# An elementwise Huber loss in larger tiles: three slots and a quarter in place of two pairs of slots

## The chip, the core and the metric

The kernel runs on one core of one Trainium2 chip. The metric is the device time of one execution in microseconds (us), lower being better. The kernel before takes 1868.55 us, the median of three runs (1867.75 to 1868.61).

## The reference

`pred` and `target` are float32 arrays of 8192 x 8192, and so is the result:

```
diff = pred - target
abs_diff = np.abs(diff)
np.where(abs_diff <= 1.0, 0.5 * diff**2, abs_diff - 0.5)
```

With m for `diff` clamped to -1 to 1, the result is also max(|diff| - 0.5, 0.5 m m); both kernels compute it in that form. Every element of two arrays is read once and every element of a third is written once: 805.3 MB in all.

## The kernel before

The arrays are flattened and seen as 128 partitions by 524288 columns in all. They are cut into tiles of 128 x 13248 (`W`, line 25); what is left over, 128 x 7616, is the first tile (lines 28 to 30). That is 40 tiles. Within a tile each partition holds one run of consecutive elements (`block`, line 34), so a row of a full tile is 52992 bytes.

On-chip memory holds two slots for `pred` (`a0`, `a1`) and two for `target` (`b0`, `b1`), each of a tile's width (lines 38 to 40). Tile i uses slot i mod 2 of each.

`load(i)` (line 49) issues the transfers of both inputs, through line 53. A middle tile has one transfer of `pred` and one of `target`. The first two tiles, and the second and third from the end, have their loads cut in two halves; the last has four quarters of each (lines 55 to 62). `store(i)` (line 67) writes the result from the `target` slot through line 70, in one transfer, and the last tile's in five. All transfers, loads and stores, are issued by SP, in the order in which the program states them. SP waits at each for what it needs: the store for the last result, a load for its slot.

`compute(i)` (line 72) cuts a middle tile into three pieces of 4416 columns. For each piece there are five instructions:

- line 92, DVE: a = a - b
- line 93, DVE: b = a clamped to -1 to 1
- line 96, ACT: b = 0.5 b b (a square with a scale)
- line 97, ACT: a = |a|
- line 86, DVE: b = max(a - 0.5, b), put off until two further pieces have been started (`finish(2)`), the last of a tile after its last piece

The order on each engine is that of the program text (`manual_schedule`, line 102). The main loop computes tile i, issues its store, and then the loads of tile i + 2 into the same slots (lines 104 to 110):

```
load(0)
load(1)
for i in range(n):
    compute(i)
    store(i)
    if i + 2 < n:
        load(i + 2)
```

The load of `pred` i + 2 needs slot `a` of tile i, whose last reader is line 86 of tile i. The load of `target` i + 2 needs slot `b` of tile i, whose last reader is the store of tile i, so SP waits there until that store has landed.

Of the kernel before, what the change touches and what calls it, by code (L numbers as in the profile page):

```python
# [1 line left out]

# [4 lines left out]


@with_exitstack
def kernel(  # L10
    ctx: ExitStack,
    tc: tile.TileContext,
    pred: bass.AP,
    target: bass.AP,
    out: bass.AP,
):
    nc = tc.nc
    P = 128
    fp32 = mybir.dt.float32
    Alu = mybir.AluOpType  # L20
    Act = mybir.ActivationFunctionType
    SQRT_HALF = 0.70710678118654752

    total = pred.shape[0] * pred.shape[1] // P
    W = 13248
    H, Q, E = W // 2, W // 4, W // 8

    widths = [W] * (total // W)
    if total % W:
        widths.insert(0, total % W)  # L30
    n = len(widths)
    starts = [sum(widths[:i]) * P for i in range(n)]

    def block(x, i):
        flat = x.rearrange("r m -> (r m)")
        return flat[starts[i] : starts[i] + P * widths[i]].rearrange("(p m) -> p m", p=P)

    pool = ctx.enter_context(tc.tile_pool(name="slots", bufs=1))
    a_slots = [pool.tile([P, W], fp32, name=f"a{k}") for k in range(2)]
    b_slots = [pool.tile([P, W], fp32, name=f"b{k}") for k in range(2)]  # L40

    def cuts(pieces):
        at, found = 0, []
        for w in pieces:
            found.append(slice(at, at + w))
            at += w
        return found

    def load(i):
        a, b = a_slots[i % 2], b_slots[i % 2]  # L50

        def get(dst, src, c):
            nc.sync.dma_start(out=dst[:, c], in_=block(src, i)[:, c])  # L53

        if i == n - 1:
            c = cuts([Q] * 4)
            order = [(0, 0), (0, 1), (1, 0), (1, 1), (0, 2), (1, 2), (0, 3), (1, 3)]
            for which, k in order:
                get((a, b)[which], (pred, target)[which], c[k])
            return  # L60
        w = widths[i]
        pieces = [w // 2] * 2 if i in (0, 1, n - 3, n - 2) else [w]
        for c in cuts(pieces):
            get(a, pred, c)
            get(b, target, c)

    def store(i):
        pieces = [Q] * 3 + [E] * 2 if i == n - 1 else [widths[i]]
        for c in cuts(pieces):
            nc.sync.dma_start(out=block(out, i)[:, c], in_=b_slots[i % 2][:, c])  # L70

    def compute(i):
        if i == n - 1:
            pieces = [E] * 8
        elif i == n - 2:
            pieces = [Q] * 4
        elif i == 0:
            pieces = [widths[0] // 2] * 2
        else:
            pieces = [W // 3] * 3  # L80
        todo = []

        def finish(keep):
            while len(todo) > keep:
                a, b = todo.pop(0)
                nc.vector.scalar_tensor_tensor(  # L86
                    out=b, in0=a, scalar=-0.5, in1=b, op0=Alu.add, op1=Alu.max
                )

        for c in cuts(pieces):  # L90
            a, b = a_slots[i % 2][:, c], b_slots[i % 2][:, c]
            nc.vector.tensor_tensor(out=a, in0=a, in1=b, op=Alu.subtract)  # L92
            nc.vector.tensor_scalar(  # L93
                out=b, in0=a, scalar1=-1.0, scalar2=1.0, op0=Alu.max, op1=Alu.min
            )
            nc.scalar.activation(out=b, in_=b, func=Act.Square, scale=SQRT_HALF)  # L96
            nc.scalar.activation(out=a, in_=a, func=Act.Abs)  # L97
            todo.append((a, b))
            finish(2)
        finish(0)  # L100

    ctx.enter_context(tc.manual_schedule())

    load(0)
    load(1)
    for i in range(n):
        compute(i)
        store(i)
        if i + 2 < n:
            load(i + 2)  # L110


# [1 line left out]
_INS = ['pred', 'target']  # L114
_OUTS = [((8192, 8192), 'float32')]


# [23 lines left out]
```

## Time and profile before

| what | value |
|---|---|
| median of 3 runs | 1868.55 us |
| span of the profiled execution, first to last instruction | 1867.4 us |
| DVE busy | 1406.2 us, 75% |
| ACT busy | 903.9 us, 48% |
| bytes moved, and mean rate over the span | 805.37 MB, 431 GB/s |
| transfers issued by SP | 138 |
| packets, counting one per partition row and one per transfer and DMA engine that signals its end | 19879, 2208 of them under 512 B |

For the profiled execution the profile gives the span of its instructions and no time of its own beside it, so the 1.15 us between the span and the median of the other runs is carried along as a constant.

The 138 transfers fit the packets: 138 x 128 rows are 17664, 138 x 16 engines are 2208, and 7 packets fetch instructions.

How to read it: the second part of the page cuts the span into 40 slices and shows the busy share of each engine and of the 16 DMA engines. Where one row is full in every slice, that row sets the time, and the others show how much cover there is. The timeline lists instructions in order of time; an instruction of the form `SPq ... DMA_DIRECT2D` is the moment at which SP hands a transfer to the DMA engines, not the transfer itself. The idle time in square brackets at an instruction names what ended it.

### The profile page before, as it was taken

How to read it: one execution, taken by the hardware profiler on the slowest of the kernel's cores; microseconds unless marked ns; L12 is line 12 of the kernel's file. 1: busy time of each engine (PE TensorE's matmuls, PEld its weight loads, DVE VectorE, ACT ScalarE, POOL GpSimd, SP SyncE). 2: the span in 40 equal slices, each digit the busy share in tenths (PEclk: the TensorE clock that was granted, in tenths of full speed). 3: DMA queues.
4: the chain of work that ended last, by engine and by line, in shares of the span. 5: the costliest groups of instructions: out<-in, count | busy, mean ns of one | idle time of the engine just before them, and what ended most of it. 6: DMA issues, size and time to landing. Idle time of an engine off the chain costs nothing.

```text
span 1867.4 us, 994 instructions
## 1 busy us (share of the span) xinstructions
DVE 1406.2 (75%) x375; ACT 903.9 (48%) x251; POOL 0.2 (0%) x4
## 2 busy tenths in 40 slices
DVE  5677777777777777777777777777777777777886
ACT  3444444444444444444444444444444444444454
POOL 0000000000000000000000000000000000000000
DMA  9999999999999999999999999999999999999999
GB/s 412 423 432 436 436 431 433 436 432 431 428 435 434 435 432 432 432 435 434 434 434 435 432 434 432 435 434 432 436 434 432 434 434 432 432 436 430 432 429 390
DMA packets 19879, 805.37 MB, mean 431 GB/s; under 512 B 2208, under 2 KB 2208, under 8 KB 2464
## 3 DMA queue, kind: packets, MB, share of 16 engines
q1 hardware_dynamic: 19872, 805.32, 99.9%
q14 instruction: 7, 0.06, 0.0%
HBM read 536.87 MB, written 268.44 MB: 431 GB/s over the span
## 4 chain that ended last, share of the span: by engine, by line
DMA 61%; DVE 37%; issue 0%; SPq 0%; DVEq 0%
DMA b<-in_target_dram 33%; DMA out_dram<-b 28%; DVE b L86 15%; DVE a L92 15%; DVE b L93 8%; SPq L53 0%; DVEq L136 0%; DVEq L92 0%
## 5 line engine op out<-in xcount | busy, mean ns | idle before, releaser
L96 ACT ACTIVATE b<-b 128x4416 f32<-128x4416 f32 (+3 forms) x125 | 461.1, 3688 | 945.6 <-DVE b L93 945.6
L92 DVE TENSOR_TENSOR a<-a,b 128x4416 f32<-128x4416 f32 (+3 forms) x125 | 565.4, 4523 | 439.2 <-DMA b<-in_target_dram 439.2
L86 DVE SCALAR_TENSOR_TENSOR b<-a,b 128x4416 f32<-128x4416 f32 (+3 forms) x125 | 558.6, 4521 | 2.7 <-ACT a L97 2.7
L97 ACT ACTIVATE a<-a 128x4416 f32<-128x4416 f32 (+3 forms) x125 | 460.3, 3682 | 0.0
L93 DVE TENSOR_SCALAR b<-a 128x4416 f32<-128x4416 f32 (+3 forms) x125 | 293.1, 2344 | 4.3
L96 ACT ACT_TABLE_LOAD x1 | 1.3, 1283 | 0.7 <-PEq L125 0.7
L125 POOL MEMSET const-bfloat16-1.0<- 128x1 bf16 x1 | 0.1, 102 | 0.0
L125 POOL MEMSET const-uint8-127<- 128x1 uint8 x1 | 0.1, 101 | 0.0
L125 POOL MEMSET const-float32-0.0<- 128x1 f32 x1 | 0.1, 99 | 0.2 <-issue 0.2
L125 POOL MEMSET const-float32-1.0<- 128x1 f32 x1 | 0.1, 98 | 0.0
## 6 DMA issues: line engine op xcount, KB each, us to landing
out_dram<-b SPq DMA_DIRECT2D x38, 6624.0 KB, 26.9
a<-in_pred_dram SPq DMA_DIRECT2D x35, 6624.0 KB, 42.1
b<-in_target_dram SPq DMA_DIRECT2D x35, 6624.0 KB, 31.3
a<-in_pred_dram SPq DMA_DIRECT2D x6, 3312.0 KB, 30.4
b<-in_target_dram SPq DMA_DIRECT2D x6, 3312.0 KB, 30.5
a<-in_pred_dram SPq DMA_DIRECT2D x4, 1656.0 KB, 31.6
b<-in_target_dram SPq DMA_DIRECT2D x4, 1656.0 KB, 18.6
out_dram<-b SPq DMA_DIRECT2D x3, 1656.0 KB, 18.9
```

What stands on the lines that cost most here:

```text
L86: nc.vector.scalar_tensor_tensor(out=b, in0=a, scalar=-0.5, in1=b, op0=Alu.add, op1=Alu.max)
L92: nc.vector.tensor_tensor(out=a, in0=a, in1=b, op=Alu.subtract)
L93: nc.vector.tensor_scalar(out=b, in0=a, scalar1=-1.0, scalar2=1.0, op0=Alu.max, op1=Alu.min)
L96: nc.scalar.activation(out=b, in_=b, func=Act.Square, scale=SQRT_HALF)
L97: nc.scalar.activation(out=a, in_=a, func=Act.Abs)
L125: nc = _bacc.Bacc("TRN2", target_bir_lowering=False, num_devices=1)
```

## The change

The tiles become 128 x 16256 (`W` = 4 `Q`, `Q` = 4064), 31 of them, with a first tile of 13568 columns and a last of 6784: 33 tiles. On-chip memory is one buffer of 3 `W` + `Q` columns. `target` (and the result) of even tiles lies at 0, of odd tiles at `W`. There is one region for `pred`, at 2 `W` for even tiles and `Q` columns further for odd ones, so that the `pred` regions of neighbouring tiles overlap in three quarters. The first tile's `pred` lies at `W`, where the `target` of tile 1 comes later.

The subtraction now writes into the `target` region (`d` = pred - target there). For a middle tile all four subtractions, 4064 columns each, come first (`subtract_all`), the quarter that no later transfer needs last. Then SP may load the next `pred` tile over the freed region, and the rest of the tile, eight pieces of 2032 columns (`loss`), works in the `target` region and in a quarter that is free meanwhile (`scratch`), which has room for two clamped pieces. Line 100 (the former line 86) is put off by one piece (`finish(1)`), not two.

For a middle tile the built program has SP wait, ahead of the load of the next `pred`, for the third of the four subtractions: for tile 1 these are the instructions 25 to 28 that DVE signals, and SP waits for 27. The order on SP is: store of tile i - 1, `pred` of i + 1, `target` of i + 1. That `target` load still waits until the store of tile i - 1 has landed. Transfers are 108 in number: 4 loads each for the first and the last two tiles, 2 for each of 30 others, and 36 stores.

```diff
-    W = 13248
+    Q = 4064
+    W = 4 * Q
+    middle = 31
+    first = 13568
+    widths = [first] + [W] * middle + [total - first - middle * W]
...
+    mem = pool.tile([P, 3 * W + Q], fp32, name="mem")
+    def at_a(i):
+        if i == 0:
+            return W
+        if i == n - 1:
+            return at_a(n - 2)
+        return 2 * W + (Q if i % 2 else 0)
+    def at_b(i):
+        return W if i % 2 else 0
+    def scratch(i):
+        following = min(i + 1, n - 2)
+        return 2 * W if at_a(following) != 2 * W else 3 * W
...
+    def subtract(i, c):
+        a, b = view(at_a(i), c), view(at_b(i), c)
+        nc.vector.tensor_tensor(out=b, in0=a, in1=b, op=Alu.subtract)
...
+    def loss(i, c):
+        finish(1)
+        d = view(at_b(i), c)
+        t = view(scratch(i) + turn[0] * (Q // 2), (0, c[1] - c[0]))
+        turn[0] ^= 1
+        nc.vector.tensor_scalar(
+            out=t, in0=d, scalar1=-1.0, scalar2=1.0, op0=Alu.max, op1=Alu.min
+        )
+        nc.scalar.activation(out=t, in_=t, func=Act.Square, scale=SQRT_HALF)
+        nc.scalar.activation(out=d, in_=d, func=Act.Abs)
+        todo.append((d, t))
...
+    def subtract_all(i):
+        order = [1, 2, 3, 0] if at_a(i) == 2 * W else [0, 1, 2, 3]
+        for k in order:
+            subtract(i, (k * Q, k * Q + Q))
...
     load(0)
-    load(1)
-    for i in range(n):
-        compute(i)
-        store(i)
-        if i + 2 < n:
-            load(i + 2)
+    load_pred(1, (0, W))
+    work_on_part(0, 0)
+    work_on_part(0, 1)
+    finish(0)
+    load_target(1, (0, W))
+    for i in range(1, n - 2):
+        store(i - 1)
+        subtract_all(i)
+        load(i + 1)
+        for c in cuts(even(W, 8)):
+            loss(i, c)
+        if i < n - 3:
+            finish(0)
+    work_on_part(n - 2, 0)
+    store(n - 3)
+    load(n - 1)
+    work_on_part(n - 2, 1)
+    work_on_part(n - 1, 0)
+    store(n - 2, even(W, 2))
+    work_on_part(n - 1, 1)
+    finish(0)
+    h = 1696
+    store(n - 1, [widths[n - 1] // 2, widths[n - 1] // 2 - h, h])
```

`work_on_part(i, k)` subtracts and treats half k of a tile piece by piece (pieces of 1696 columns in the first and last tile, of 2032 in the last but one); the tiles at both ends are worked so. The last tile is stored in 3392, 1696 and 1696 columns.

## The prediction

> **What bounds it now.** I read the page first: busy shares by slice and the chain that ended last.
>
> ```profile
> DVE  5677777777777777777777777777777777777886
> ACT  3444444444444444444444444444444444444454
> POOL 0000000000000000000000000000000000000000
> DMA  9999999999999999999999999999999999999999
> GB/s 412 423 432 436 436 431 433 436 432 431 428 435 434 435 432 432 432 435 434 434 434 435 432 434 432 435 434 432 436 434 432 434 434 432 432 436 430 432 429 390
> ...
> DMA 61%; DVE 37%; issue 0%; SPq 0%; DVEq 0%
> ```
>
> The DMA row is full in all 40 slices, while DVE is never above 8 tenths. The chain names DVE for 37%, but only because store and load hang on it in turn; a full DMA row means that the queue held other work meanwhile. The timeline of one steady tile shows this:
>
> ```profile
> 602.43 0.34 SPq L70 DMA_DIRECT2D out_dram<-b  x1
> 602.91 0.34 SPq L53 DMA_DIRECT2D a<-in_pred_dram  x1
> 613.83 4.76 DVE L92 TENSOR_TENSOR a<-a,b 128x4416 f32<-128x4416 f32 x1 [11.42 <-DMA b<-in_target_dram]
> ...
> 629.41 0.33 SPq L53 DMA_DIRECT2D b<-in_target_dram  x1
> ...
> 649.44 0.34 SPq L70 DMA_DIRECT2D out_dram<-b  x1
> 650.27 0.33 SPq L53 DMA_DIRECT2D a<-in_pred_dram  x1
> 660.77 4.76 DVE L92 TENSOR_TENSOR a<-a,b 128x4416 f32<-128x4416 f32 x1 [11.35 <-DMA b<-in_target_dram]
> ```
>
> The store is issued 11.4 us before the target load ahead of it has landed (602.43, 613.83); the wait for the store ends at 629.41, 15.58 us after that landing, and pred is already queued. From landing to landing (613.83 to 660.77) three transfers take 46.94 us, 15.647 each, with no gap. So only three things can move the time: what each transfer costs beside its bytes, gaps that the new order opens, and both ends.
>
> **Price of a transfer.** The start shows a smaller size:
>
> ```profile
> 0.73 0.37 SPq L53 DMA_DIRECT2D a<-in_pred_dram  x1
> ...
> 12.55 4.12 DVE L92 TENSOR_TENSOR a<-a,b 128x3808 f32<-128x3808 f32 x1 [12.55 <-DMA b<-in_target_dram]
> ...
> 21.62 4.13 DVE L92 TENSOR_TENSOR a<-a,b 128x3808 f32<-128x3808 f32 x1 [2.76 <-DMA b<-in_target_dram]
> ```
>
> Two transfers of 3808 columns take 21.62 - 12.55 = 9.07 us, 4.535 each. With 15.647 us for 13248 columns, a column costs 11.112 us / 9440 = 1.1771 ns and a transfer 0.05 us more. The same rows price a start from an empty queue: 12.55 - 9.07 = 3.48, which is 2.75 us from the first issue (0.73) to where transfer time begins, counting the way to DVE at the landing.
>
> All columns cost 3 x 524288 x 1.1771 ns = 1851.4 us; 138 transfers add 6.9; the start is 3.48; after the data the span goes on some 0.9 us (the last packets fall in 1865 to 1866, by windows of 1 us). Together 1862.7. The span is 1867.4, so 4.7 us are stalls of the slowest DMA engine. They lie early: the five pairs of tiles between the target issues at 110.37 and 582.48 (chain of waits) take 472.1 us, the five after it (582.48 to 1051.80) 469.3, that is 0.28 us more per tile.
>
> **The change, part by part.**
>
> *Fewer transfers.* 138 become 108: 30 x 0.05 = **-1.5 us**. On the full queue nothing hides this.
>
> *Early stalls.* The trace does not say what makes them. If they come per tile, 33 tiles for 40 leave 4.7 x 33/40 = 3.9, **-0.8 us**; bounds: all vanish (-4.7), or the early 0.28 us for each of 33 tiles (9.2, +4.5). I take -0.8, nearest to what this order of load and store showed.
>
> *The new wait.* Now pred i + 1 cannot queue until three subtractions of tile i are done; the queue then holds only the store of i - 1. Prices by these rows:
>
> ```profile
> L92 DVE TENSOR_TENSOR a<-a,b 128x4416 f32<-128x4416 f32 x111 | 527.7, 4754 | 413.9 <-DMA b<-in_target_dram 413.9
> ...
> L92 DVE TENSOR_TENSOR a<-a,b 128x1656 f32<-128x1656 f32 x8 | 15.0, 1876 | 2.5 <-DMA b<-in_target_dram 2.5
> L86 DVE SCALAR_TENSOR_TENSOR b<-a,b 128x1656 f32<-128x1656 f32 x8 | 14.8, 1876 | 0.0
> ...
> L96 ACT ACTIVATE b<-b 128x1656 f32<-128x1656 f32 x8 | 12.6, 1579 | 17.9 <-DVE b L93 17.9
> ...
> L93 DVE TENSOR_SCALAR b<-a 128x1656 f32<-128x1656 f32 x8 | 8.2, 1022 | 0.3
> ```
>
> Line 92 grows by (4754 - 1876) / 2760 = 1.043 ns a column, so 4064 columns take 4.39 us; independent neighbours overlap by 0.085 (line 86, three of 4.752 in 14.09). Three take 13.0 us. A queue start behind that: 13.0 + 2.75 = 15.75 us after the landing of target i. The store queued there takes 16256 x 1.1771 ns + 0.05 = 19.19 us. **Slack 3.4 us per tile, cost 0.** Without this cover each us is paid 30 times. The wait of target i + 1 for the store's landing is covered by pred i + 1, 19.19 us against 2.75.
>
> Queued on SP ahead of that load is the store of i - 1, which waits for DVE. The pieces of 2032 columns cost, by 1656 and the slope of their other rows, 1.22 (line 93), 2.27 (line 86) and 1.89 us (lines 96, 97, each). DVE needs 17.3 + 8 x 3.3 = 43.8 us a tile. ACT paces the pieces: 8 x 3.65 = 29.2, so the tile ends 17.3 + 1.2 + 29.2 + 2.3 = 50 us after its target landed. The store must be queued by 57.6 - 2.75 = 54.8: slack 4.8. More instructions on DVE and ACT thus cost 0.
>
> *Start.* Part loads of 6784 columns take 8.04 us: 19.55 and 35.6 for the two halves. The subtractions of the second half end, with their neighbours (four of line 91 at 1.85, three of line 100 at 1.85, three of line 110 at 1.04), at 51.7. Then target 1 may queue: 54.45 against the end of pred 1 at 35.6 + 19.19 = 54.8. Pred 2: target 1 lands at 74.0, + 15.75 = 89.7, against the end of the first store (13568 columns, 16.02 us) at 90.0. Both have 0.3 us to spare: cost 0, bounds 0 to 2 us once.
>
> *End.* The last target load waits for the landed store of n - 3, covered by a pred part of 4.04 us (needs 2.75). The last pieces are 1696 columns, before 1656: 0.
>
> **Sum:** -1.5 - 0.8 = -2.3: span 1865.1, and with the 1.15 us that the median stands above the profiled span, **1866.3 us**.
>
> **Rivals.**
>
> *A wait takes the place of the cover (slower).* Behind a busy queue the start was never seen, only behind an empty one (2.75). The new wait decides from 3.4 us beyond that, 6.2 us in all: at 7.2 it is +30 us, 1896; and if the load waited for the fourth subtraction too, 17.3 + 2.75 - 19.19 = +0.9 a tile, +26 us, 1892. Against both: the built wait is for the third, and hand-over from DVE to SP took 0.02 us in the rows above. Chance 0.10.
>
> *Rows of 65024 bytes run slower (slower).* Pitch goes from 52992 to 65024 bytes, near 64 KiB. The slowest middle slice ran at 428 GB/s against 434; at that rate throughout: + 1.4% of 1851 = +26, 1892. For it there is nothing in this trace, since 15232-byte rows (3808 columns) and 52992-byte rows share one price. Chance 0.06. The Trainium skill ("DMA: Bandwidth & Descriptors", Latency and other measured facts) has copies slow down when rows lie large powers of two apart, 207 against 214 GB/s at a pitch of 512 KiB; by that figure this would be an estimated 3%, some 1925 us, but no run here has such a pitch, and ours is 512 bytes off a power of two.
>
> *The stalls stay at their early rate (slower).* They stopped once the run was a quarter through. If the shorter queue keeps the DMA engines in step, 0.28 a tile persists: 1868.55 - 1.5 + 4.5 = 1871.6, 1874 with both start margins lost. Chance 0.08.
>
> *The stalls vanish (faster).* 1868.55 - 1.5 - 4.7 = 1862.4. Chance 0.12.
>
> *It does not do what it says:* DMA stays full anyway and transfers were all there was to gain; that is the forecast, chance 0.64.
>
> **Numbers.** This kernel's runs differ by 0.05%; I call 0.2% (3.7 us) what a measurement tells from no change. The forecast's own range is 1864.9 to 1869, within 0.2%. The range 1863.5 to 1874 leaves out part of the vanishing stalls and the two dear rivals, under 0.2. Faster: 0.12 and a rest of 0.02, 0.14. Slower: 0.10 + 0.06, and three quarters of 0.08 taken as 0.06, 0.22. Same: 0.64.
>
> **What would show it.** DMA full in every slice after the first; 57.6 us from one first subtraction of a middle tile to the next; pred issued 13 us after the target landed, at least 3 us before the store lands; 108 transfers. A period of 58 us or more, or slices under 430 throughout, would prove it wrong.

## The result, and the profile after

The changed kernel takes 1876.91 us, the median of six runs (1870.76 to 1881.54). The kernel before, beside it, takes 1868.47 (1867.75 to 1868.65). The ratio is 1.0041, its interval 1.0031 to 1.0051: **slower by 0.41%**, 5.8 to 9.5 us, outside the forecast's range. The runs now differ by 0.6%, where those of the kernel before differ by 0.05%. The profiled execution has a span of 1879.8 us, against 1867.4 before: 12.4 us are to be found. It is the longest of the six (1881.54 us), so this is more than the 8.4 us by which the medians differ.

The page of the kernel after, its slices and its chain by engine:

```profile
DVE  5677877778777787777887777877778777787797
ACT  3166533566334664346643356533566334664375
POOL 0000000000000000000000000000000000000000
DMA  9999999999999999999999999999999999999999
GB/s 424 409 425 439 429 434 439 425 439 425 432 422 429 433 429 439 426 429 429 433 432 428 422 440 426 439 426 429 429 439 426 433 428 436 428 436 425 423 415 391
...
DMA 55%; ACT 23%; DVE 21%; issue 1%; ACTq 0%; SPq 0%; DVEq 0%
```

The DMA row is as full as before, and so doesn't tell the two kernels apart. Only the rate has moved: from the eighth slice on it was 428 to 436 in the kernel before, the last slice aside; now it swings between 422 and 440, and falls lower at the end. A DMA engine whose packet is late counts as busy, so a full row does not mean that bytes flow.

The timeline of two middle tiles of the kernel after, SP's issues and the first subtractions (start, duration, engine and line):

```profile
936.77 0.34 SPq L87 DMA_DIRECT2D out_dram<-mem  x1
945.00 17.30 DVE L91 TENSOR_TENSOR mem<-mem 128x4064 f32<-128x4064 f32 x4 [8.25 <-DMA mem<-in_target_dram]
958.06 0.33 SPq L75 DMA_DIRECT2D mem<-in_pred_dram  x1
...
964.10 0.33 SPq L78 DMA_DIRECT2D mem<-in_target_dram  x1
...
995.01 0.34 SPq L87 DMA_DIRECT2D out_dram<-mem  x1
1003.34 17.29 DVE L91 TENSOR_TENSOR mem<-mem 128x4064 f32<-128x4064 f32 x4 [8.36 <-DMA mem<-in_target_dram]
```

The schedule is the one foretold: `pred` is issued 13.06 us after the landing of `target` (945.00 to 958.06), and the store lands 6.04 us after that, at 964.10. From there `pred` and `target` should land in 2 x 19.18 = 38.36 us. They took 964.10 to 1003.34, 39.24. The tile lost 0.9 us between two loads that were both queued in time. The period is 58.34 us instead of 57.6.

The chain of waits shows the same for other tiles: each line is the stretch (start, us) from the landing of a store to that of the `target` load behind it, `pred` and `target` together. First the kernel after:

```profile
209.50 38.36 DMA mem<-in_target_dram
...
324.54 38.86 DMA mem<-in_target_dram
...
440.74 39.31 DMA mem<-in_target_dram
...
905.88 39.03 DMA mem<-in_target_dram
...
1137.74 38.45 DMA mem<-in_target_dram
```

and the kernel before:

```profile
204.31 31.68 DMA b<-in_target_dram
...
298.94 31.52 DMA b<-in_target_dram
...
393.84 32.04 DMA b<-in_target_dram
...
582.48 31.25 DMA b<-in_target_dram
...
676.35 31.23 DMA b<-in_target_dram
```

38.36 and 31.25 are the undisturbed stretches of the two kernels. Before, single stretches lose 0.3 to 0.8 us until some 480 us have passed, and none after that. After, they lose 0 to 0.95 us to the end of the run.

The trace gives more. Every transfer ends with 16 signals, one from each DMA engine. From them I use three numbers: the **spread** of a transfer, from its first signal to its last; its **loss**, the time between its last signal and that of the transfer ahead, less 1.1771 ns a column and 0.046 us (a price that fits the signals of the first part loads, of 3808 and 6784 columns, to 0.03 us); and the **lead** of a transfer, the time from its issue to the first signal of the transfer ahead. Summed losses of the profiled executions, in us:

```
          transfers   loss   first 150 us   between   last 60 us   span
before       138       5.4        1.5          3.7        0.2      1867.4
after        108      19.0        4.5         12.7        1.8      1879.8
```

The loss grew by 13.6 us, and 30 transfers fewer save 30 x 0.046 = 1.4. That leaves +12.2 of the 12.4 us seen. 13.2 of the 19.0 are lost at the end of `target` loads, 3.2 at stores, 2.6 at `pred`.

The 3.2 us at stores have a cause of their own. The pages count the packets that fetch the program's own instructions, before:

```profile
q14 instruction: 7, 0.06, 0.0%
```

and after:

```profile
q14 instruction: 10, 0.08, 0.0%
```

Such a packet of 8192 bytes holds one DMA engine for 0.31 us, and in the cases that follow the data row behind it took 0.35 to 0.7 us longer than the median. Where that engine is the last one, the whole transfer lands later. The kernel after has four jumps of 0.76 to 0.82 us at stores, landed at 500, 848, 1196 and 1602 us; they follow fetches at 484.53, 832.82, 1180.64 and 1586.24, and in three of them the rows can be followed from the fetch to the last signal (in the fourth they can't be told apart). The kernel before has one such jump, 0.61 us at 1475. Without these the middle lost 9.5 us, against 3.0 before.

### The profile page after: what moved, and what is told of

The parts are those of the page before. It is cut to its first block, busy times and chain, and to the rows that moved or that the text cites. A ratio compares the mean times of both kernels' runs of the same rounds, so it can differ in the third digit from the quotient of the medians.

```text
span 1879.8 us, 1475 instructions
## 1 busy us (share of the span) xinstructions
DVE 1455.9 (77%) x660; ACT 939.1 (50%) x521; POOL 0.2 (0%) x4
## 4 chain that ended last, share of the span: by engine, by line
DMA 55%; ACT 23%; DVE 21%; issue 1%; ACTq 0%; SPq 0%; DVEq 0%
DMA mem<-in_target_dram 33%; DMA out_dram<-mem 22%; DVE mem L91 16%; ACT mem L113 12%; ACT mem L114 11%; DVE mem L100 4%; DVE mem L110 2%; ACTq L179 0%; SPq L75 0%; SPq L78 0%; DVEq L91 0%; ACTq L113 0%
## 5 line engine op out<-in xcount | busy, mean ns | idle before, releaser
L113 ACT ACTIVATE mem<-mem 128x2032 f32<-128x2032 f32 (+1 forms) x260 | 488.0, 1877 | 928.7 <-DVE mem L110 898.5
L91 DVE TENSOR_TENSOR mem<-mem 128x4064 f32<-128x4064 f32 (+2 forms) x140 | 560.0, 4053 | 267.8 <-DMA mem<-in_target_dram 267.8
L100 DVE SCALAR_TENSOR_TENSOR mem<-mem 128x2032 f32<-128x2032 f32 (+1 forms) x260 | 587.1, 2258 | 138.9 <-ACT mem L114 134.7
L114 ACT ACTIVATE mem<-mem 128x2032 f32<-128x2032 f32 (+1 forms) x260 | 485.4, 1867 | 0.0
L110 DVE TENSOR_SCALAR mem<-mem 128x2032 f32<-128x2032 f32 (+1 forms) x260 | 311.9, 1209 | 7.9
```

The source lines that it names most:

```text
L91: nc.vector.tensor_tensor(out=b, in0=a, in1=b, op=Alu.subtract)
L100: nc.vector.scalar_tensor_tensor(out=d, in0=d, scalar=-0.5, in1=t, op0=Alu.add, op1=Alu.max)
L110: nc.vector.tensor_scalar(out=t, in0=d, scalar1=-1.0, scalar2=1.0, op0=Alu.max, op1=Alu.min)
L113: nc.scalar.activation(out=t, in_=t, func=Act.Square, scale=SQRT_HALF)
L114: nc.scalar.activation(out=d, in_=d, func=Act.Abs)
```

## The experiments

Three theories name the loss; the expectations use their letters. **Q**, the queue: `pred` comes too late, not for the slowest DMA engine, against which the prediction counted, but for the fastest; the first engine ends the store 3 to 5 us ahead of the last, so that of 3.4 us of slack nothing is left. **R**, the rows: rows of 65024 bytes lose time of themselves. **D**, the direction: the loss needs the turn from loading to storing, or back, and is not a matter of loads alone.

### The next pred tile in two halves (e1), the target in two halves (e2)

In `load`, for middle tiles, e1:

```diff
-        for c in parts.get(i, [(0, W)]):
...
+        for c in cuts([2 * Q, 2 * Q]):
             load_pred(i, c)
-            load_target(i, c)
+        load_target(i, (0, W))
```

The first half waits for fewer subtractions and is queued earlier. e2 cuts the target load instead:

```diff
-        for c in parts.get(i, [(0, W)]):
-            load_pred(i, c)
...
+        load_pred(i, (0, W))
+        for c in cuts([2 * Q, 2 * Q]):
             load_target(i, c)
```

> The changed kernel with the pred load of each middle tile cut in two halves (30 more transfers, +1.5 us). The first half then waits for one or two subtractions in place of three and is queued 4.4 to 8.8 us earlier. Theory Q (late queue): pred comes so late that the fastest DMA engines have run dry by then and lose their lead, so that all 16 turn from loading to storing close together, and the last packets of each target load stall. Then the stalls go: 1864 to 1869 us, under 40 us of stalls summed over the 16 engines against about 240. Theory R (row size): rows of 65024 bytes make the packets at the turn longer, and the stall with them. The target rows stay whole here, so 1876 to 1880 us.

> The changed kernel with the target load of each middle tile cut in two halves by columns, so that its rows have 32512 bytes, and pred as late as in the changed kernel. Theory Q (late queue): nothing about the engines' lead changes, 1875 to 1881 us with stalls at every tile. Theory R (row size): the packets at the turn are half as long and their stalls too, 1868 to 1872 us.

e1: 1872.16 us (1870.6 to 1873.88), ratio to before 1.0019 (1.0009 to 1.0028), span 1870.6. e2: 1872.2 (1871.36 to 1874.54), 1.0023 (1.0013 to 1.0032), span 1870.6. The chain of e1:

```profile
669.75 38.41 DMA mem<-in_target_dram
...
784.87 38.40 DMA mem<-in_target_dram
...
900.77 38.42 DMA mem<-in_target_dram
```

With a mean lead of 8.2 us ahead of `pred`, the middle loses 5.4 us instead of 12.7, although both have the same rows of `target` and of the store. Ten of the fifteen such stretches in its chain behind the start last 38.40 to 38.45 us, the longest 39.39. That speaks for Q, but the number missed the 1864 to 1869 expected, and the slow rows of all engines (over 0.1 us above the median) still add up to 77 us among full and half rows, against 233 in the kernel after and under 40 expected. 29 more transfers take back 1.3 us; 2.3 of the 5.4 us are three jumps at stores behind instruction fetches; and late in the run, where the spread is 5.2 to 6.3 us, the store's own lead falls to 1.7 to 2.2 us and single `target` loads lose 0.2 to 0.5 us again. e2 was meant as the control and is none: with half of `target` landed early, the subtractions begin 9.6 us earlier, so `pred` and the store are queued earlier too, with mean leads of 8.6 and 9.8 us. Its time lies where R had been expected (1868 to 1872) and below Q's 1875, but with both changed at once it can't tell the two apart.

### Smaller tiles: pred as late as now (e3), pred early (e4), stores in halves as well (e5)

e3 keeps the order of the change with `Q` at 3264, so rows of 52224 bytes, about those of the kernel before, and a shorter store to cover `pred`:

```diff
-    Q = 4064
+    Q = 3264
-    middle = 31
-    first = 13568
+    middle = 39
+    first = 10240
...
-    h = 1696
+    h = 1216
```

e4 adds a full second region for `pred`, so that the load no longer waits for subtractions of the tile at work:

```diff
-    mem = pool.tile([P, 3 * W + Q], fp32, name="mem")
+    mem = pool.tile([P, 4 * W], fp32, name="mem")
...
-        return 2 * W + (Q if i % 2 else 0)
+        return 2 * W + (W if i % 2 else 0)
...
-        following = min(i + 1, n - 2)
-        return 2 * W if at_a(following) != 2 * W else 3 * W
+        if i == 0:
+            return 2 * W
+        if i >= n - 2:
+            return 5 * W - at_a(n - 2)
+        return at_a(i)
...
-        order = [1, 2, 3, 0] if at_a(i) == 2 * W else [0, 1, 2, 3]
+        order = [0, 1, 2, 3]
```

e5 is e4 with the first half of each store issued as soon as it is computed:

```diff
-        store(i - 1)
+        store(i - 1, even(widths[i - 1], 2))
```

> The changed kernel's scheme, one pred region and a quarter, with tiles of 128 x 13056 (rows of 52224 bytes, 132 transfers). Without stalls it would take some 1865 us. The slack of the late pred load is 15.4 - 10.5 - 2.75 = 2.1 us in place of 3.4. Theory Q (late queue): stalls at every one of 39 tiles, at 0.3 to 0.5 us each, 1876 to 1886 us. Theory R (row size): as few stalls as before the change, 1865 to 1870 us.

> As the late small tiles (128 x 13056), but with two whole pred regions, so that pred needs no subtraction and is queued right behind the store of the tile before, while all subtractions of a tile still come first. Theory Q (late queue): the stalls die out early in the run as in the kernel before, 1864 to 1870 us. Theory S (the order of the work: subtractions first, store nearer to the end of the target load): stalls as in the late small tiles, 1876 to 1886 us. Theory R (row size): 1864 to 1870 us.

> The early small tiles (128 x 13056, two pred regions, all subtractions first) with the store of each middle tile cut in two halves, so that its first half is queued some 12 us earlier than the whole store was; 170 transfers, some 1866.5 us without stalls. In the early small tiles the store was issued only 1 to 2 us before the fastest DMA engines had finished the target load. Theory Q, widened to any transfer at a change of direction (a transfer that is queued late lets the fastest engines run dry, which puts all 16 back in step, and the next change of direction stalls): the stalls go, 1868 to 1872 us. Theory S (all subtractions first): the stalls stay, 1888 to 1892 us.

| | median (range), us | ratio to before | span | loss: all, middle |
|---|---|---|---|---|
| e3 | 1912.86 (1906.14 to 1918.12) | 1.0236 (1.0212 to 1.026) | 1910.6 | 48.5, 38.4 |
| e4 | 1888.6 (1887.27 to 1888.92) | 1.0107 (1.0092 to 1.0122) | 1886.7 | 24.6, 18.8 |
| e5 | 1875.26 (1874.19 to 1877.66) | 1.0037 (1.0024 to 1.005) | 1872.8 | 8.9, 3.0 |

The DMA rows of e3's page:

```profile
DMA  9999999999999999999999999999999999999999
GB/s 411 389 432 423 419 421 422 420 425 426 421 421 423 429 423 421 425 431 421 421 430 425 421 420 427 424 425 420 426 422 428 420 434 422 421 429 424 421 415 384
```

e3 settles R: with shorter rows the loss in the middle is three times as large, and not as small as before the change. Its lead at `pred` is 1.17 us, and a tile loses 0.96 us at the end of its `target` load. That is two to three times the 0.3 to 0.5 us that Q had expected; the direction was right, the size was not.

e4 was to cure it and did not. Q as I had put it, for `pred` alone, falls here: `pred` leads by 17.5 us. But the store now comes late: it waits for the whole computation, and its mean lead is 2.1 us. The chains, e4 first, then e5:

```profile
539.35 31.48 DMA mem<-in_target_dram
...
632.50 31.77 DMA mem<-in_target_dram
...
726.32 31.45 DMA mem<-in_target_dram
```

```profile
538.52 30.76 DMA mem<-in_target_dram
...
631.04 30.75 DMA mem<-in_target_dram
...
723.55 30.75 DMA mem<-in_target_dram
```

With the store in halves the same stretch is 30.75 to 30.81 us in all but two lines of the chain's middle (31.08 and 31.04), and the middle loses 3.0 us instead of 18.8, though e5 has 38 transfers more. So what Q says of `pred` holds for a late store as well. e5 still misses its 1868 to 1872: 2.8 us are lost at its start, 3.1 in its last 60 us, and its 170 transfers cost 1.5 more than 138.

### A load in the place of each store (e6)

```diff
-        store(i - 1)
+        load_in_place_of_store(i - 1)
...
-    store(n - 3)
+    load_in_place_of_store(n - 3)
```

```
def load_in_place_of_store(i):
    c = (0, widths[i])
    nc.sync.dma_start(out=view(at_b(i), c), in_=block(pred, i)[:, c[0] : c[1]])
```

The results of all tiles but the last two are not written. Bytes, order and waits stay: the load of `pred` goes over the place that the store would have read. The next `pred` is issued 6.06 us ahead of that transfer's landing, where it was 6.04.

> The changed kernel with every store of a tile but those of the last two tiles replaced by a load of the same size into the same place, at the same point of the queue; the results of those tiles are not written. All waits are as in the changed kernel, and the DMA engines only load. Theory D (the stall needs a change from loading to storing or back): nearly no stalls, 1862 to 1866 us. Rival B (engines in step stall at any boundary between two transfers): 1872 to 1880 us as in the changed kernel.

Measured: 1870.05 us (1869.0 to 1871.68), ratio 1.0008 (0.9999 to 1.0017), span 1869.3. The chain of e6:

```profile
182.22 26.63 DMA mem<-in_pred_dram
208.87 38.37 DMA mem<-in_target_dram
...
297.35 26.64 DMA mem<-in_pred_dram
324.00 38.39 DMA mem<-in_target_dram
...
412.50 26.65 DMA mem<-in_pred_dram
439.16 38.39 DMA mem<-in_target_dram
```

From 208 us on every `target` stretch is 38.37 to 38.40: in the middle of the run the ends of `target` loads lose 0.6 us in all, in the kernel after some 10. The leads at `pred` are not quite the same, though: the spread is smaller here, so their mean is 3.1 us instead of 2.4. But in the six tiles whose lead was 1.7 to 2.6 us `target` lost 0.01 to 0.03 us each, where sixteen tiles of the kernel after with leads of 1.4 to 2.5 lost 0.46 on average. So the loss at the end of `target` loads needs a store behind it: D holds. The total missed the 1862 to 1866 expected, since 3.8 us go at the start and 3.6 in the middle; 2.3 of the latter are three loads, at 843, 1189 and 1593 us, whose last engine had an instruction fetch in its way.

### Three regions and a half (e7)

With `Q` at 3712 there is room to set the `pred` regions two quarters apart, so that the load waits for two subtractions and not three, and the fourth subtraction follows the first two pieces of the loss:

```diff
-    Q = 4064
+    Q = 3712
-    middle = 31
-    first = 13568
+    middle = 34
+    first = 12928
...
-    mem = pool.tile([P, 3 * W + Q], fp32, name="mem")
+    mem = pool.tile([P, 3 * W + 2 * Q], fp32, name="mem")
...
-        return 2 * W + (Q if i % 2 else 0)
+        return 2 * W + (2 * Q if i % 2 else 0)
...
-        order = [1, 2, 3, 0] if at_a(i) == 2 * W else [0, 1, 2, 3]
-        for k in order:
+        order = [2, 3, 0, 1] if at_a(i) == 2 * W else [0, 1, 2, 3]
+        for k in order[:3]:
...
```

> Tiles of 128 x 14848 (rows of 59392 bytes, 117 transfers) in three slots and a half: pred of the next tile waits for two subtractions in place of three, and the larger free half lets two clamps start ahead of the fourth subtraction, so that the store is queued earlier too. Pred and store are then queued 8 to 9 us before the slowest engine needs them, in place of 3.4 and some 7. Some 1863.5 us without stalls. Theory Q: stalls early in the run alone, 1865 to 1868.5 us. If the scheme with one pred region or rows above 52992 bytes are what stalls: 1872 us or more.

Measured: 1873.34 us (1871.5 to 1874.18), ratio 1.0025 (1.0016 to 1.0035), span 1869.6. Leads are 5.9 us at `pred` and at the store. In the profiled execution, the shortest of the ten, the losses behave as in the kernel before: `target` loads of the middle lose nothing after 703 us, and of the 4.6 us in the middle 1.5 are two jumps at stores behind fetches (8.3 us in all). So the new kind of loss is gone in this execution; but what was to be gained, 21 transfers at 0.046 us, is 1.0 us, and 2.9 us more are lost than before. The expected 1865 to 1868.5 was too hopeful.

### Pred in halves, both late (e10)

e1 with the two halves issued in the other order, so that the first issued waits as long as the whole tile did:

```diff
-        for c in cuts([2 * Q, 2 * Q]):
+        for c in cuts([2 * Q, 2 * Q])[::-1]:
             load_pred(i, c)
```

> Control for the pred halves: the same two halves of pred, but the second half is issued first, and it needs the third subtraction, so that both halves are queued as late as the whole pred of the changed kernel. 138 transfers, some 1864.5 us without stalls. Theory Q (a late transfer puts the DMA engines in step): stalls at every tile as in the changed kernel, 1874 to 1883 us. If it was the shorter transfers that helped and not the earlier queueing: 1870 to 1873 us as with the pred halves.

Measured: median 1871.79 us, ten runs from 1869.42 to 1879.35, ratio 1.0027 (1.0015 to 1.0038). Inconclusive. The profiled execution (1872.11 us, near the median) had leads of 2.5 to 3.4 us at the first half of `pred` and lost 2.4 us in the middle; by these leads it was less late than the kernel after, with its 1.4 to 3.1. The median lies where the rival had been expected, that shorter transfers help and not earlier queueing, and below Q's 1874. What the run does show is the width: early halves gave 1870.6 to 1873.88, late halves 1869.42 to 1879.35, like the kernel after (1870.76 to 1881.54). With leads near 3 us the time was a matter of chance. Whether shorter rows of `pred` help as well stays open.

### The kernel before, with its DMA engines set apart at the start (e9, e11, e12, e13)

If the early losses of the kernel before come while the 16 engines still turn together, engines that are apart from the start should lose nothing. e9 gives some engines more to do than others, by part loads of 8, 4, 2 and 1 partitions ahead of `load(0)`; e11 the same into four places:

```diff
+    for rows in (8, 4, 2, 1):
+        nc.sync.dma_start(out=a_slots[1][:rows, 0:H], in_=block(pred, 1)[:rows, 0:H])
     load(0)
```

```diff
+    places = [(a_slots[1], 0), (a_slots[1], H), (b_slots[1], 0), (b_slots[1], H)]
+    for rows, (slot, at) in zip((8, 4, 2, 1), places):
+        nc.sync.dma_start(out=slot[:rows, at : at + H], in_=block(pred, 1)[:rows, 0:H])
     load(0)
```

> The kernel before with four extra loads of 8, 4, 2 and 1 partitions (6624 columns each) ahead of all others, which are not used; each DMA engine that takes one row of them starts 1 us later, so that up to eight engines are 1 to 4 us behind the rest from the start. Theory Q: engines that are not in step do not stall, so the sum of the stalls over 16 engines falls from 58 us to under 35, and the time changes by 0 to +4 us (1868 to 1872). If the early stalls have another cause than engines in step, the sum stays near 58 us and the time is 1872 us.

> The kernel before with four extra loads ahead of all others, of 8, 4, 2 and 1 partitions (6624 columns each, not used), now into four places that do not overlap, so that none waits for another. Up to eight DMA engines get 1 to 4 rows of 1 us more than the rest and start the work that much later. Theory Q: engines that are not in step stall less: the slowest engine loses under 3 us to stalls in place of 5, and the time is 1867 to 1871 us, 4 us of extra loads included. If engines in step are not the cause, the loss stays at 5 us and the time is 1872 to 1874 us.

e9: 1882.46 us, ratio 1.0074 (1.0058 to 1.0091), span 1880.7. It was badly made: the four loads have one destination, and each waited for the one before, as SP's line shows (four issues in 14.37 us):

```profile
0.73 14.37 SPq L105 DMA_DIRECT2D a<-in_pred_dram  x4
```

e11: 1873.95 us (1873.68 to 1877.35), ratio 1.0033 (1.002 to 1.0046), span 1871.9. Its first subtraction, in the timeline, and its chain:

```profile
22.35 4.12 DVE L92 TENSOR_TENSOR a<-a,b 128x3808 f32<-128x3808 f32 x1 [22.35 <-DMA b<-in_target_dram]
```

```profile
212.44 31.26 DMA b<-in_target_dram
...
306.29 31.26 DMA b<-in_target_dram
...
400.12 31.25 DMA b<-in_target_dram
...
493.94 31.26 DMA b<-in_target_dram
```

The start costs 9.8 us (22.35 against 12.55), more than the 4 I had reckoned. But behind it the stretches that lost 0.3 to 0.8 us before (204 to 394) are now 31.25 to 31.26. Summed over full rows and all 16 engines, packets that took over 0.1 us longer than the median add up to 3.2 us, against 35.5 in the kernel before. The spread is 4.4 to 4.8 us from the start. And the rest of the run, 1871.9 - 9.8 = 1862.1, is 5.3 us shorter than the 1867.4 before: all but 0.1 of the 5.4 us of loss (0.6 of them the fetch at 1475 us, which in e11 does not fall on the last engine). This is the clearest of these runs: the early stalls of the kernel before go when its engines are apart. In e9, too, the slow full rows add up to less than before, 16.7 us; over rows of all sizes, which the expectation meant with its 58, they come to 61, because its start adds to them.

e12 and e13 tried to get the spread at no cost, by cutting one load of the second tile by partitions, in the kernel before:

```diff
...
+            if (i, k) == (1, 0):
+                for lo, hi in ((0, 112), (112, 120), (120, 128)):
+                    nc.sync.dma_start(out=a[lo:hi, c], in_=block(pred, i)[lo:hi, c])
+            else:
+                get(a, pred, c)
```

and in e13 `(0, 112), (112, 120), (120, 124), (124, 128)`.

> The kernel before, all data loaded and stored, with one of its early loads (pred of the second tile, first half) cut by partitions into 112, 8 and 8. The transfers of 8 partitions go to half of the DMA engines, which so get 9 rows in place of 8, the other half 7: from then on the two halves are some 2 us apart, and the slower half carries one row (1.0 us) more than its share. Theory Q (engines in step stall at a change of direction): the stalls summed over the engines fall from 35 us to under 12, the slowest engine saves 3 to 4 us for a price of 1.1: 1865 to 1867 us. If two halves of eight engines in step stall as before: 1869 us.

> As the two groups, but with 112, 8, 4 and 4 partitions: 4 engines get 10 rows, 4 get 8 and 8 get 7, three groups 1 and 3 us apart; the slowest carry two rows (2.0 us) more than their share. Theory Q: stalls under 8 us summed over the engines, 4 to 5 us saved for a price of 2.1: 1865 to 1867 us. If the spread does not matter: 1870 us.

e12: 1880.58 us, ratio 1.006 (1.0046 to 1.0073). e13: 1884.6, 1.0083 (1.0069 to 1.0097). e12's timeline, at the second half of the second tile:

```profile
64.73 4.76 DVE L96 TENSOR_TENSOR a<-a,b 128x4416 f32<-128x4416 f32 x1 [8.41 <-DMA b<-in_target_dram]
```

The same subtraction starts at 53.65 in the kernel before: 11.1 us are lost at once, not the 1.1 expected. Rows of 26496 bytes took up to 4.0 us there, instead of 0.98. In e13 it is 15.3 us. The prices at the start decide both times. The slow rows by sum are 23.7 us in e12, nearly all between 150 and 500 us, and 2.4 in e13. Yet e13's run behind that subtraction takes 1813.9 us, as long as the kernel before (1813.7) and not 4 to 5 us less. Its trace shows where the time went: the `target` loads of the middle lose 0.2 us instead of 3.2, as expected, but three stores, landed at 266, 877 and 1488 us, lose 0.8 each behind an instruction fetch, and 2.2 us are lost at part loads of the last tiles.

## Why the prediction was wrong

**The transfers** were right: 108 were issued, 30 fewer at 0.046 us each. **The durations** were right: four subtractions 17.3 us, `pred` issued 13.06 us after the landing (13.0), the store issued 8.23 us ahead of the landing (57.6 - 50 = 7.6). The group view of the kernel after:

```profile
L100 DVE SCALAR_TENSOR_TENSOR mem<-mem 128x2032 f32<-128x2032 f32 x248 | 564.1, 2274 | 136.2 <-ACT mem L114 132.0
L91 DVE TENSOR_TENSOR mem<-mem 128x4064 f32<-128x4064 f32 x120 | 518.9, 4385 | 247.5 <-DMA mem<-in_target_dram 247.5
L113 ACT ACTIVATE mem<-mem 128x2032 f32<-128x2032 f32 x248 | 468.6, 1889 | 891.1 <-DVE mem L110 860.8 <-issue 28.6
L114 ACT ACTIVATE mem<-mem 128x2032 f32<-128x2032 f32 x248 | 466.2, 1880 | 0.0
L110 DVE TENSOR_SCALAR mem<-mem 128x2032 f32<-128x2032 f32 x248 | 299.4, 1218 | 7.5
```

4385, 2274, 1889, 1880 and 1218 ns stand against 4.39, 2.27, 1.89 and 1.22 us. More and smaller pieces on DVE and ACT cost nothing on these engines, as said. But the program has 1475 instructions instead of 994, and in the profiled execution the fetches that fell on a last engine cost 3.2 us instead of 0.6; the sum had no term for that.

**"Rows of 65024 bytes run slower"** did not come: an undisturbed pair of loads takes 38.36 us, the 2 x 19.18 of the old price per column, and e3 lost more with shorter rows. The Trainium skill ("DMA: Bandwidth & Descriptors", Latency and other measured facts) has copies slow down at a row pitch of 512 KiB and more. No run here has such a pitch, and at 64 KiB less 512 bytes nothing of it is seen.

**"The new wait ... Slack 3.4 us per tile, cost 0"** is the step that failed. It set 15.75 us against the 19.19 us after which the store has landed, and a store has landed when the *last* of 16 engines is done. At 964 us the first engine was done with the store at 960.12 and the last at 964.08. `pred` was issued at 958.06, a lead of 2.06 us, and with the 2.75 us of a start that is 0.7 us late for the first engine. The trace does not show a gap there: the packets of the next load begin at once, but on the first five engines they take 2.47 to 2.88 us instead of 2.40. The step is wrong in its kind and not only in its size: the slack that counts is the lead. The Trainium skill ("DMA: Bandwidth & Descriptors", Queues, rings and completion order) has each DMA engine drain a ring of its own, and the 16 signals here do end 3 to 5 us apart.

With it the losses of the middle, fetches aside, rose from 3.0 to 9.5 us, and the mean period is 58.0 us where 57.6 had been expected. Most of this is lost one turn later. At 995.9 to 998.7 us the last row of the `target` load on each of the 16 engines took 2.68 to 3.83 us, where 2.40 is the median; that is the 0.9 us of the stretch from 964.10. Sorted by the lead of `pred`, mean time lost by all 16 engines in slow rows around the turn, in us per middle tile:

```
                        tiles   lead       store to pred   target to store
after, lead under 2.6     16    1.4-2.5         2.2              7.8
after, lead 2.6 to 5      12    2.6-3.1         0.4              1.8
e3                        36    mean 1.2        6.6              7.6
e7                        31    mean 5.9        0.0              0.3
before                    35    mean 23         0.1              0.6
e4 (the store is late)    36    mean 17.5       4.6              1.8
```

In the kernel after `pred` is issued some 6 us ahead of the store's last signal in nearly every tile, so there a short lead is the same thing as a large spread of the store (correlation -0.91). It takes the other runs to tell the two apart: e7 has the spread of the kernel after (3.6 us on average, against 3.7), a longer lead and little loss. The limit lies near the 2.75 us of a start, which the prediction had in hand. e4 is the mirror of the others in this sum: there the store is the late transfer, and more of the time goes at the turn that follows the store. By the last signals, which set the time, e4 too loses at the end of `target` loads, 15.8 of the 18.8 us of its middle.

**"Early stalls ... -0.8"** failed with it. The 4.7 us were taken as a sum per run or per tile, and the trace "does not say what makes them". e11 and e6 tell more: in the kernel before the losses go when its engines are apart, and in the new order they need a store behind the loads. The new order calls them up in every part of the run. Also, the 1.15 us added at the end is no constant of the kernel: each run on record stands 1.7 to 2.1 us above its own span, so the profiled execution before was itself some 0.6 us longer than the median.

**"Start ... cost 0, bounds 0 to 2 us once"** failed in the same way. The issues came as foretold, 51.87 for 51.7 and 88.26 for 87.0 plus what was lost by then:

```profile
51.87 0.33 SPq L78 DMA_DIRECT2D mem<-in_target_dram  x1
...
88.26 0.33 SPq L75 DMA_DIRECT2D mem<-in_pred_dram  x1
```

The 0.3 us "to spare" were counted against the slowest engine; the three loads there lost 1.2, 2.1 and 1.1 us.

**"End ... 0"** was wrong by 1.6 us. It looked at the wait of the last `target` load alone. But the store of n - 3 was itself issued 0.6 us after the first engine had ended the load ahead of it, and two of the part loads behind it lost 1.0 and 0.8 us.

**The rival "The stalls stay at their early rate"** named this: "If the shorter queue keeps the DMA engines in step". It had a chance of 0.08 and an end at 1874; the median is 1876.9. Its rate was 0.28 us a tile; the middle tiles lost 0.36 at `target` alone. The sign that was to show a step wrong, a period of 58 us or more, came.

**What stays open** is how a late `pred` makes a turn stall that comes 40 us later. "In step" fits the kernel before, whose stalls end when its spread has grown from 0.6 to 3.4 us, and e11. It also fits the rows at 960 us: the nine engines that ended the store first did so within 0.8 us, and ended their next row within 0.5. But it is not seen in the spread: over the middle of the kernel after it is 3.7 us on average, more than the 3.3 of the kernel before. From tile to tile the loss at `target` hardly goes with the store's spread (correlation 0.1), and the time in slow rows goes with it the wrong way: tiles with a larger spread lose more, at the store-to-`pred` turn (0.82) and at the next (0.63). The time lost at the one turn goes with that at the other (0.61). That a short lead brings the stalls is shown, by e3, e5 and e7, where whole `pred` transfers or the store come later or sooner, and by e1; the way from the one to the other is argued. e10 leaves open how much shorter transfers do of themselves.

No version here beats the kernel before. The 5.4 us that its DMA engines lose are all that there was to gain beside the transfers, and e11 gained nearly all of them, at a start that costs 9.8.

## What to carry to other kernels

Where the DMA queue is the bound, count the slack of a late issue from the first engine's end of the transfer ahead, not from its landing: here that takes 3 to 5 us off, and where loads and stores took turns a mean lead of 1.2 to 2.4 us cost 0.4 to 1 us a tile (e3, e4 and the kernel after). When a wait is moved off one transfer, look for the next one that is issued late (e4), and if it can't come sooner as a whole, issue a part of it sooner (e1, e5). Read the rate beside the busy share: a stalled packet counts as busy. Before a loss is put down to the queue, look whether an instruction fetch fell on the engine that was last.

## What was not expected of the hardware

- The 16 DMA engines drift apart: the spread of a transfer grows from 0.6 us to 3.4 us by 480 us in the kernel before, to 4.2 at its end. Apart from the start (e11), they lost next to nothing in that kernel: 31.25 us a stretch instead of up to 32.04.
- A fetch of instructions, 8192 bytes, takes its turn on one DMA engine among the data. Where that engine was the last, the store landed 0.8 us later (the kernel after at 1586 us, e13 at 255, 866 and 1477 us).
- The turn from loading to storing cost up to 1.4 us on a row of 2.40 us, on all 16 engines at once (996 us in the kernel after). With loads alone (e6) the ends of the same loads lost 0.6 us in the whole middle of the run.
- On a full queue a transfer costs 0.046 us beside its bytes; from an empty one 2.75 us. The step between the two is not sharp: in the kernel after, with leads of 1.4 to 3.1 us in its profiled execution, the time varies from run to run by 0.6%.
- A load cut by partitions (112, 8 and 8) moves its rows slowly: 26496 bytes in up to 4.0 us instead of 0.98 (e12).
